# Two DeepNorm layers on one core: where the sums of the feed-forward weights are made

## The chip, the cores and the metric

The kernel runs on one core of one Trainium2 chip. The metric is the device time of one execution in microseconds. Five engines run their own instruction streams in order: PE (TensorE, matmuls), DVE (VectorE), ACT (ScalarE), POOL (GpSimd) and SP (SyncE, which issues most transfers). Sixteen DMA engines, shared by all queues, move data between HBM and on-chip memory. The two queues that matter here are q1 (transfers that SP issues) and q0 (transfers that POOL issues).

## The reference

Two layers over 1024 latent and 256 context tokens, width 1024. Each layer is a modulated input projection, three head groups (latent attention, differential attention, chunk mixing), an output projection with a LayerNorm residual, and a gated feed-forward part with a convolution over three tokens:

```
def conv_ffn(h, p):
    u = dwconv3(h @ p["ffn_wup"], p["ffn_convw"], p["ffn_convb"])
    gate, val = jnp.split(u, 2, axis=-1)
    return (jax.nn.silu(gate) * val) @ p["ffn_wdown"]
...
def layer(x, xc, mod, modc, rows, cols, p, layer_idx, need_ctx):
    ...
    y, yc = mixer(x * (1.0 + sc1) + sh1, xc * (1.0 + csc1) + csh1, rows, cols, p, layer_idx, need_ctx)
    x = layer_norm(DN_ALPHA * x + g1 * y, p["ln1_g"], p["ln1_b"])
    x = layer_norm(DN_ALPHA * x + g2 * conv_ffn(x * (1.0 + sc2) + sh2, p), p["ln2_g"], p["ln2_b"])
```

`ffn_wup` is 1024 x 5632, `ffn_wdown` is 2816 x 1024, all in float32. Layer 1 leaves the context tokens out of its output and feed-forward parts.

## The kernel before

**Numbers.** Each float32 operand is split into a high part (`hi`, type fp32r) and the rest (`lo`), and a product is three matmuls: hi·hi, hi·lo, lo·hi (`mm3`). `split` makes `hi` by a copy on ACT (L460) and `lo` by a subtraction on DVE or POOL (L457).

**The feed-forward part in seven products.** Up and down projections are 2 x 2 block products done with seven block products in place of eight (a Strassen-like scheme), so that sums of weight blocks are needed beside the blocks. For the up projection there are 22 column blocks f (`NF`), and in each the four quarters of the weight, 128 x 512 each, are called 11, 12, 21, 22; S1 = 21 + 22, S2 = S1 + 11, S3 = 21 + 11, S4 = 12 + S2. The products use 11, 12, S1, S2, S3, S4 and 22 (and 21 in layer 0, for the context tokens). For the down projection there are 11 pairs (`NP`) and four sums as well.

**Sums made by transfers.** Before, all of these sums are made in HBM by transfers that POOL issues on q0. `sums` lists them for one layer: a sum of a chunk is a plain copy of one operand (L592) and then a transfer that adds the other operand to what lies there (L593, `accum_op`). Each is 1408 KB, cut in rows of 8 KB for the adding one (176 rows, `SUMROWS`); the sums are called `ws` (up) and `db` (down). `begin_sums` takes the next one of the list and hands it to the planner. This happens in the input projection (`in_chunk`, every fourth tile), among the fillers of the attention (`program`), and in the up phase (`ffn`, L1811). The ws of layer 0 are started in the input projection and the attention of layer 0; the db of layer 0 and half of the ws of layer 1 in the up phase of layer 0; the rest of these in the input projection and the attention of layer 1; the db of layer 1 in the up phase of layer 1.

**The up phase.** For each block f, `up_load` loads the seven or eight weight tiles of 256 KB by SP (L444), four of them from `ws`; `up_operand` splits each on ACT and DVE, `UP_LOOK` = 4 tiles ahead of the product; `up_slot` runs the products on PE and combines them: DVE reads PSUM at L1640 (S2), L1650 (S3) and L1654 (S4), ACT copies the others, and `conv` runs on ACT (L1671) and DVE (L1673). Once in two blocks `store_pair` writes seven combinations of the result to HBM (`da`, `dc`), made by `comb` (L1490) on DVE or POOL. L1650 runs once in each block, so its starts count the blocks.

**What sets the order.** All work goes into `Sched` as tasks with a priority (the order of writing plus `key`), the engines that may take it and a cost; a list scheduler plans it with its own estimates and thereby fixes the order in each engine's stream and the on-chip places ("region" tiles). A POOL transfer counts 1.0 us there and lands 40 us later. On the chip each engine then runs its stream in order and waits by semaphores.

## Time and profile before

| what | value |
| --- | --- |
| median of 3 runs | 3523.48 us (3515.53 to 3527.67) |
| profiled execution | 3522.21 us, its span 3520.4 us |
| granted TensorE clock, mean | 0.957 |
| PE, DVE, ACT, POOL busy | 91%, 73%, 47%, 30% of the span |
| input projection of layer 0, attention | to about 300 us, 300 to 980 us |
| up phase of layer 0, down phase | 985 to 1680 us, 1680 to 2010 us |
| input projection of layer 1, attention | 2010 to 2200 us, 2200 to 2770 us |
| up phase of layer 1, down phase | 2770 to 3257 us, 3257 us to the end |

The span is from the first to the last instruction; the run's time is 1.8 us longer. An instruction's row says which engine ran it, on which line, what it wrote and read, and how long it took; a wait's row says which engine stood still and what ended that. "PE idle" is taken from the rows of PE that carry a wait in brackets. PEclk in a stretch is the TensorE clock that was granted, as a share of full speed; a share of 0.5 is the lower of two levels.

### The profile page before, as it was taken

The numbers are of one execution on the slowest core, as the hardware profiler recorded it, in microseconds if no ns is written. First come the engines' busy times: TensorE is split into PE (matmuls) and PEld (weight loads), VectorE is DVE, ScalarE is ACT, GpSimd is POOL, SyncE is SP. The second block draws the span as 40 slices with busy tenths as digits, with TensorE's granted clock in tenths as the row PEclk, the third lists the DMA queues.
The fourth block names the chain that finished last, engine by engine and source line by source line (L and its number), as shares of the span: only waits on it lengthen the run. The fifth ranks groups of instructions, "written<-read, shape, count | busy, mean of one in ns | idle before, by whom it ended". The sixth has DMA issues, their size and how long they took to land. (4 is left out here: it accounts for less than half of the span.)

```text
span 3520.4 us, 53639 instructions
## 1 busy us (share of the span) xinstructions
PE 3210.6 (91%) x18953; PEld 2801.2 (80%) x18953; DVE 2586.0 (73%) x6262; ACT 1652.2 (47%) x2931; POOL 1045.3 (30%) x678
## 2 busy tenths in 40 slices
PE   7799999998988889989998899999998889999997
PEld 5798888787977777777886799888888867788775
DVE  7456988988777566657569737889898776666687
ACT  5024666565344344434435404566663445454543
POOL 3101555553122111213034301454434232212143
PEclk9899999999999999999999999999998999999998
DMA  8823444443345666664765743132313556653672
GB/s 324 206 65 100 116 120 131 120 106 104 111 145 168 191 176 181 191 173 147 225 217 188 213 130 78 49 77 82 89 53 121 163 157 200 201 163 132 222 263 102
DMA packets 274839, 528.07 MB, mean 150 GB/s; under 512 B 67465, under 2 KB 119177, under 8 KB 264585
## 3 DMA queue, kind: packets, MB, share of 16 engines
q1 hardware_dynamic: 263048, 386.22, 34.1%
q0 software_dynamic: 11520, 138.42, 15.9%
q8 instruction: 149, 2.44, 0.3%
q14 instruction: 122, 0.99, 0.1%
HBM read 444.25 MB, written 218.69 MB: 188 GB/s over the span
## 5 line engine op out<-in xcount | busy, mean ns | idle before, releaser
L447 PE MATMUL t<-region 128*128 128x256 f32 (+4 forms) x15631 | 2876.0, 342 | 233.4 <-DVE region L457 69.7
L447 PEld LDWEIGHTS t<-region 128*128 128x128 f32 x15631 | 2458.0, 194 | 584.9 <-DVE region L457 82.6
L457 DVE TENSOR_TENSOR region<-region 128x512 fp32r<-128x512 f32 (+6 forms) x867 | 765.2, 907 | 267.8 <-ACT region L460 225.0
L460 ACT ACTIVATE region<-t 128x512 fp32r<-128x512 f32 (+4 forms) x935 | 452.6, 511 | 717.1 <-PE t L447 326.0
L460 ACT ACTIVATE region<-region 128x512 fp32r<-128x512 f32 (+4 forms) x944 | 591.2, 662 | 384.8 <-PE t L447 131.9
L457 POOL TENSOR_TENSOR region<-region 128x512 fp32r<-128x512 f32 (+5 forms) x289 | 403.9, 1408 | 1123.2 <-ACT region L460 804.6
L1490 POOL TENSOR_TENSOR region<-region 128x512 f32<-128x512 f32 (+2 forms) x107 | 212.0, 1984 | 911.3 <-ACT region L460 355.2
L1673 DVE SCALAR_TENSOR_TENSOR region<-region,conv 128x1023 f32<-128x1023 f32 x176 | 233.4, 1327 | 165.6 <-ACT region L1671 165.3
L1198 ACT ACTIVATE region<-region,q 128x1280 f32<-128x1280 f32 (+1 forms) x216 | 273.5, 1267 | 165.2 <-DVE q L1197 148.7
L1193 DVE TENSOR_SCALAR_CACHE_REDUCE region<-t 128x512 f32<-128x512 f32 (+1 forms) x600 | 333.6, 586 | 9.4 <-PE t L447 8.0
L457 DVE TENSOR_TENSOR region<-t,region 128x512 fp32r<-128x512 f32 (+1 forms) x529 | 297.8, 598 | 46.4 <-ACT region L460 41.6
L1262 PE MATMUL t<-ident,region 128*128 128x128 f32 x1312 | 186.1, 285 | 19.9 <-DVE region L1193 5.0
L1238 POOL TENSOR_TENSOR region<-region 128x1280 f32<-128x1280 f32 (+1 forms) x69 | 188.4, 2731 | 5.8
L1262 PEld LDWEIGHTS t<-ident,region 128*128 128x128 f32 x1312 | 154.9, 147 | 27.6 <-DVE region L1193 8.2
L1671 ACT ACTIVATE region<-region,conv 128x1024 f32<-128x1024 f32 x88 | 109.2, 1241 | 128.2 <-DVE region L1654 56.7
L1237 POOL TENSOR_SCALAR region<-region,q 128x1280 f32<-128x1280 f32 (+1 forms) x69 | 87.4, 1267 | 205.6 <-DVE q L1232 128.2
L447 PE MATMUL t<-region,s 128*4 128x256 f32 x768 | 118.2, 291 | 17.2 <-ACT region L460 10.8
L1490 DVE TENSOR_TENSOR region<-region 128x512 f32<-128x512 f32 (+2 forms) x150 | 113.3, 760 | 18.4 <-POOL region L1490 15.3
L1018 DVE TENSOR_TENSOR region<-t,region 128x256 f32<-128x256 f32 x32 | 13.6, 424 | 126.5 <-PE t L447 69.6
L447 PEld LDWEIGHTS t<-region,s 128*4 128x4 f32 x768 | 64.8, 87 | 46.4 <-ACT region L460 11.3
L548 POOL TENSOR_TENSOR region<-region 128x1024 f32<-128x1024 f32 x26 | 72.8, 2815 | 93.3 <-DMA region<-n 65.6
L1688 ACT ACTIVATE region<-region 128x1024 f32<-128x1024 f32 x66 | 53.4, 839 | 63.9 <-DVE region L1673 63.9
(137 smaller groups left out, 1849.5 us busy)
## 6 DMA issues: line engine op xcount, KB each, us to landing
ws<-in_wup POOLq DMA_DIRECT2D x48, 1408.0 KB, 9.8
region<-ws SPq DMA_DIRECT2D x176, 256.0 KB, 3.7
region<-in_ada_w SPq DMA_DIRECT2D x160, 256.0 KB, 3.5
region<-in_wup SPq DMA_DIRECT2D x154, 256.0 KB, 3.0
da<-region SPq DMA_DIRECT2D x154, 256.0 KB, 3.7
region<-da SPq DMA_DIRECT2D x154, 256.0 KB, 4.0
db<-in_w_down POOLq DMA_DIRECT2D x24, 1408.0 KB, 8.5
ws<-ws POOLq DMA_DIRECT2D x16, 1408.0 KB, 14.3
```

The lines of the kernel that those rows point to most:

```text
L447: self.nc.tensor.matmul(ps, a, b, start=start, stop=stop, skip_group_check=again)
L457: eng.tensor_tensor(out=out, in0=full, in1=hi.bitcast(F32), op=ALU.subtract)
L460: self.nc.scalar.activation(out, in_, AF.Copy, **kw)
L548: self.task(engs or pool_t(D), lambda e, row=row, op=op: self.vec[e].tensor_tensor(out=x[:, :D], in0=x[:, :D], in1=row.t, op=op), [x, row] ...
L1193: self.task(dve_t(b - a), lambda e: nc.vector.tensor_scalar(p[:, a:b], ps[:, :b - a], -scale, None, op0=ALU.mult, op1=ALU.min, accum_out=n ...
L1198: self.task(act_t(nk, 0.19), lambda e: nc.scalar.activation(p[:, :nk], p[:, :nk], AF.Exp, bias=m.t, scale=-1.0, accum_out=s.t), [p, m], [p ...
L1237: nc.gpsimd.tensor_scalar(p2[:, :nk], p2[:, :nk], cc.t, 0.0, op0=ALU.mult, op1=ALU.add)
L1238: nc.gpsimd.tensor_tensor(out=p1[:, :nk], in0=p1[:, :nk], in1=p2[:, :nk], op=ALU.add)
L1262: nc.tensor.transpose(ps[:, u, j * P:(j + 1) * P], B[key][j][:, (kt + u) * P:(kt + u + 1) * P], self.ident)
L1490: self.task(either(n), lambda e: self.vec[e].tensor_tensor(out=o(), in0=a(), in1=b(), op=op), r, w, **kw)
L1671: self.task(act_t(n, 0.15), lambda e: nc.scalar.activation(t.t, u(0, n), AF.Identity, scale=c[:, 1:2], bias=c[:, 3:4]), r + ["conv"], [t])
L1673: self.task(dve_t(n - 1, extra=0.06), lambda e, d=d: nc.vector.scalar_tensor_tensor(t[:, 1 - d:n - d], u(d, n - 1 + d), c[:, 2 * d:2 * d + ...
```

## The change

The sums of the up projection's weights are no longer made in HBM: `ws` is gone. `up_load` loads the four quarters of each block once (11 and 12 as before; 21 and 22 when S1 is due), and `up_operand` makes S1 to S4 by four additions of 128 x 512 on DVE (`comb`, which is L1480 in the changed file), keeping the quarters and the sums S1 and S2 on chip until their last use. The split of each operand is as before. The down projection's sums are still made by transfers from POOL, now in rows of 2 KB (704 rows in a transfer of the same 1408 KB, for the plain copies too), all 16 of a layer among the fillers of that layer's attention. The room for POOL's descriptors is doubled (`dynamic_dma_scratch_size`).

```diff
-SUMROWS = 176
+SUMROWS = 704
...
     def flat(self, x, c):
-        return x.rearrange("n p c -> (n p c)").rearrange("(r c) -> r c", c=2048)[c * SUMROWS:(c + 1) * SUMROWS]
+        return x.rearrange("n p c -> (n p) c")[c * SUMROWS:(c + 1) * SUMROWS]
...
-            out.append(lambda: self.s.add({"pool": 1.0}, lambda e: self.nc.gpsimd.dma_start(out=put(), in_=self.flat(a(), c)), (), **kw))
-            out.append(lambda: self.s.add({"pool": 1.0}, lambda e: self.nc.gpsimd.dma_start(out=put(), in_=self.flat(b(), c), accum_op=ALU.add, max_dma_last_dim=8192), [*r, key], **kw))
-        for c in range((NF if which == "ws" else NP) * P * 512 // (SUMROWS * 2048)):
-            at = lambda n: (which, l, n, c)
-            if which == "ws":
-                make(0, c, w(1, 0), w(1, 1))
-                make(2, c, w(1, 0), w(0, 0))
-                make(1, c, w(0, 0), lambda: x[0], [at(0)])
-                make(3, c, w(0, 1), lambda: x[1], [at(1)])
-            else:
-                make(0, c, w(0, 0), w(0, 1))
...
+            out.append(lambda: self.s.add({"pool": 1.0}, lambda e: self.nc.gpsimd.dma_start(out=put(), in_=self.flat(a(), c), max_dma_last_dim=2048), (), **kw))
+            out.append(lambda: self.s.add({"pool": 1.0}, lambda e: self.nc.gpsimd.dma_start(out=put(), in_=self.flat(b(), c), accum_op=ALU.add, max_dma_last_dim=2048), [*r, key], **kw))
+        for c in range(NP * P // SUMROWS):
+            at = lambda n: ("db", l, n, c)
+            make(0, c, w(0, 0), w(0, 1))
+            make(1, c, w(0, 1), w(1, 1))
+            make(2, c, w(1, 1), lambda: x[0], [at(0)])
+            make(3, c, w(1, 0), lambda: x[2], [at(2)])
...
-        for n, t in enumerate(tiles):
-            if name != "z" and n % 4 == 1:
-                self.begin_sums(1)
+        for t in tiles:
...
     def up_load(self, l, m):
-        while len(self.up_raw) <= min(m, len(self.up_ops) - 1):
-            f, n = self.up_ops[len(self.up_raw)]
-            raw = self.S(F32, (P, HALF))
-            if n[0] == "S":
-                j = int(n[1]) - 1
-                src, r = self.ws[l][j, f], self.sum_chunks("ws", l, j, f)
-            else:
-                src, r = self.i["wup"][l, int(n[0]) - 1, int(n[1]) - 1, f], []
-            self.dma(lambda raw=raw: raw.t, lambda src=src: src, 4 * P * HALF, r, [raw])
-            self.up_raw.append(raw)
+        while self.up_loaded <= min(m, len(self.up_ops) - 1):
+            f, n = self.up_ops[self.up_loaded]
+            self.up_loaded += 1
+            for g, h in {"11": [(0, 0)], "12": [(0, 1)], "S1": [(1, 0), (1, 1)]}.get(n, ()):
+                raw = self.S(F32, (P, HALF))
+                self.dma(lambda raw=raw: raw.t, lambda f=f, g=g, h=h: self.i["wup"][l, g, h, f], 4 * P * HALF, (), [raw])
+                self.up_raw[f, g, h] = raw
...
-        raw, self.up_raw[m] = self.up_raw[m], None
-        self.blocks[f][n] = self.parts(HALF, lambda: raw.t, [raw], engs=dve_t(HALF))
+        b = self.blocks[f]
+        raw = lambda g, h: self.up_raw[f, g, h]
+        if n[0] == "S":
+            x, y = {"S1": lambda: (raw(1, 0), raw(1, 1)), "S2": lambda: (b["s1"], raw(0, 0)), "S3": lambda: (raw(1, 0), raw(0, 0)), "S4": lambda: (raw(0, 1), b["s2"])}[n]()
+            t = b[n.lower()] = self.S(F32, (P, HALF))
+            self.comb(HALF, lambda: t.t, lambda: x.t, lambda: y.t, ALU.add, [x, y], [t], engs=dve_t(HALF))
+        else:
+            t = raw(int(n[0]) - 1, int(n[1]) - 1)
+        b[n] = self.parts(HALF, lambda: t.t, [t], engs=dve_t(HALF))
...
-        assert not self.due
-        self.due = self.sums(l, "db") + (self.sums(1, "ws") if l == 0 else [])
...
-            if f >= 2 and (x[1] == "22" or l == 0 and f % 2 and x[1] == "S2"):
-                self.begin_sums(1)
...
-        self.due = self.sums(0, "ws")
         for l in range(DEPTH):
...
+            self.due = self.sums(l)
...
-    nc = _bacc.Bacc("TRN2", target_bir_lowering=False, num_devices=1, dynamic_dma_scratch_size=1024)
+    nc = _bacc.Bacc("TRN2", target_bir_lowering=False, num_devices=1, dynamic_dma_scratch_size=2048)
```

The next three places show what the planner made of it. The first is POOL's stream in the middle of the up phase of layer 0. L1490 (L1480 in the changed file) is an addition or subtraction of `comb`, L592 the plain copy of a sum and L593 the adding transfer. Before:

```order
L1490 TENSOR_TENSOR region<-region 128x1024
L1490 TENSOR_TENSOR region<-region 128x512
L593 DMA db<-db 176x2048
L1490 TENSOR_TENSOR region<-region 128x1024
L592 DMA ws<-in_wup 32x11264
L593 DMA db<-db 176x2048
L1490 TENSOR_TENSOR region<-region 128x1024
L1490 TENSOR_TENSOR region<-region 128x512 x2
L592 DMA ws<-in_wup 32x11264
L593 DMA ws<-in_wup 176x2048
```

The same place now:

```order
L1480 TENSOR_TENSOR region<-region 128x128
L1480 TENSOR_TENSOR region<-region 128x512 x2
L1480 TENSOR_TENSOR region<-region 128x1024 x2
L1480 TENSOR_TENSOR region<-region 128x128
L1480 TENSOR_TENSOR region<-region 128x512 x2
```

No transfer is left in POOL's stream between the start of the up phase and the next attention, and of the combinations of `store_pair` POOL takes one of 128 columns more in a pair of blocks and fewer of 512.

The second place is DVE's stream in the same phase, from the combination S4 of one block (L1654, now L1648) to the splits for the next. L1673 (now L1667) is the convolution and L457 the `lo` part of an operand. Before:

```order
L1654 TENSOR_TENSOR region<-region,t 128x512
L1673 SCALAR_TENSOR_TENSOR region<-region,conv 128x1023
L1673 SCALAR_TENSOR_TENSOR region<-t,conv,region 128x255
L1673 SCALAR_TENSOR_TENSOR region<-region,conv 128x1023
L1673 SCALAR_TENSOR_TENSOR region<-t,conv,region 128x255
L457 TENSOR_TENSOR region<-region 128x512 x2
L1673 SCALAR_TENSOR_TENSOR region<-region,conv 128x1023
```

Now:

```order
L1648 TENSOR_TENSOR region<-region,t 128x512
L1480 TENSOR_TENSOR region<-region 128x512
L1667 SCALAR_TENSOR_TENSOR region<-region,conv 128x1023
L1667 SCALAR_TENSOR_TENSOR region<-t,conv,region 128x255
L1667 SCALAR_TENSOR_TENSOR region<-region,conv 128x1023
L1667 SCALAR_TENSOR_TENSOR region<-t,conv,region 128x255
L457 TENSOR_TENSOR region<-region 128x512
L1480 TENSOR_TENSOR region<-region 128x512
L457 TENSOR_TENSOR region<-region 128x512
L1480 TENSOR_TENSOR region<-region 128x512
```

The additions stand in the gaps between convolution and splits, two to four places ahead of the split that reads them; in each block DVE has 8 splits as before and 4 more instructions of this kind.

The third place is POOL's stream in the attention of layer 1. L1237 and L1238 (now L1227 and L1228) join the two maps of the differential attention. Before:

```order
L1237 TENSOR_SCALAR region<-region,q 128x1280
L1238 TENSOR_TENSOR region<-region 128x1280
L593 DMA ws<-ws 176x2048
L457 TENSOR_TENSOR region<-region 128x512 x3
L457 TENSOR_TENSOR region<-region 128x2x2x32 x2
```

Now:

```order
L1227 TENSOR_SCALAR region<-region,q 128x1280
L1228 TENSOR_TENSOR region<-region 128x1280
L592 DMA db<-in_w_down 704x512
L591 DMA db<-in_w_down 704x512
L457 TENSOR_TENSOR region<-region 128x768
L457 TENSOR_TENSOR region<-region 128x512 x2
```

From the first filler to the last, this attention has 16 transfers in POOL's stream where it had 4, and in a few places, as here, two stand one behind the other.

## Rows read from the trace of the kernel before

**Rows 1.** The page: the queue of POOL's transfers (packets, MB, share of 16 engines' span), and the issues of POOL and of the up phase's loads (how many, size of each, median time from issue to landing).

```profile
q0 software_dynamic: 11520, 138.42, 15.9%
...
ws<-in_wup POOLq DMA_DIRECT2D x48, 1408.0 KB, 9.8
region<-ws SPq DMA_DIRECT2D x176, 256.0 KB, 3.7
region<-in_wup SPq DMA_DIRECT2D x154, 256.0 KB, 3.0
db<-in_w_down POOLq DMA_DIRECT2D x24, 1408.0 KB, 8.5
ws<-ws POOLq DMA_DIRECT2D x16, 1408.0 KB, 14.3
db<-db POOLq DMA_DIRECT2D x8, 1408.0 KB, 13.0
```

**Rows 2.** Windows, one row a stretch: its length, busy time of PE, its weight loads, DVE, ACT and POOL with the number of instructions, then the granted clock, the DMA engines' busy share and GB/s. They are: the stall in the input projection of layer 0, the attention of layer 0, the up phase of layer 0 (the part with sums under way, then the part after the last of them), the up phase of layer 1 (its opening, then the rest).

```profile
150.00:170.00 20.00, 3.07 (x27) 2.87 (x25) 0.00 (x0) 0.00 (x0) 2.09 (x3) 0.64 1.04 258
300.00:980.00 680.00, 628.13 (x4524) 570.06 (x4523) 578.88 (x1813) 391.50 (x762) 281.83 (x198) 0.96 0.41 116
1094.00:1580.00 486.00, 432.53 (x2168) 363.68 (x2167) 290.38 (x367) 189.02 (x305) 86.11 (x60) 0.95 0.65 185
1580.00:1651.00 71.00, 66.50 (x343) 55.79 (x342) 50.72 (x61) 32.98 (x55) 14.96 (x8) 1.00 0.40 124
2797.00:2900.00 103.00, 84.38 (x385) 70.31 (x385) 73.24 (x80) 49.38 (x82) 32.79 (x20) 0.88 0.61 176
2900.00:3257.00 357.00, 350.01 (x1505) 281.73 (x1504) 237.83 (x275) 177.84 (x266) 73.83 (x36) 1.00 0.57 174
```

**Rows 3.** The instructions of L1650, one in each block of the up phase, in four stretches: count, shortest, median and longest duration in ns, start of the first and of the last. The stretches are 1094 to 1580 and 1600 to 1655 (layer 0), 2890 to 3260 and 3085 to 3240 (layer 1).

```profile
L1650 DVE SCALAR_TENSOR_TENSOR region<-t,region x17: 682/686/692, 1094.3 to 1570.5; 128x512 f32<-128x512 f32 x17
...
L1650 DVE SCALAR_TENSOR_TENSOR region<-t,region x3: 691/692/692, 1600.8 to 1651.0; 128x512 f32<-128x512 f32 x3
...
L1650 DVE SCALAR_TENSOR_TENSOR region<-t,region x19: 682/684/692, 2897.2 to 3256.8; 128x512 f32<-128x512 f32 x19
...
L1650 DVE SCALAR_TENSOR_TENSOR region<-t,region x8: 682/684/685, 3102.2 to 3238.9; 128x512 f32<-128x512 f32 x8
```

**Rows 4.** The timeline of one block of the up phase of layer 0, POOL, ACT, DVE and PE in turn: start, busy time, instruction, and in brackets the engine's idle time before it and what ended that.

```profile
1290.28 2.40 POOL L1490 TENSOR_TENSOR region<-region 128x1024 f32<-128x1024 f32 x1 [23.27 <-ACT region L460]
1292.63 0.55 POOL L592 DMA_DIRECT2D ws<-in_wup  x1
1293.17 0.93 POOL L593 DMA_DIRECT2D db<-db  x1
...
1307.63 0.63 ACT L460 ACTIVATE region<-region 128x512 fp32r<-128x512 f32 x1 [9.56 <-DMA region<-in_wup]
...
1290.44 2.78 DVE L457 TENSOR_TENSOR region<-region 128x512 fp32r<-128x512 f32 x1
...
1308.29 0.69 DVE L457 TENSOR_TENSOR region<-region 128x512 fp32r<-128x512 f32 x1 [10.91 <-ACT region L460]
...
1309.64 10.55 PE L447 MATMUL t<-region 128*128 128x512 f32 x52 [7.09 <-DVE region L1650]
```

**Rows 5.** Waits in the input projection of layer 0, 110 to 175 us: who waited for whom, us in total, how often, the longest.

```profile
DVE region L1018 <- DMA zd<-region: 39.8, 1, 39.8
POOL ws L593 <- issue: 24.8, 4, 7.8
...
PE t L447 <- DVE region L1024: 19.4, 1, 19.4
```

**Rows 6.** The timeline where the input projection of layer 1 begins, POOL, ACT and PE in turn, columns as in rows 4.

```profile
1992.47 0.96 POOL L593 DMA_DIRECT2D ws<-in_wup  x1
...
2006.87 0.84 ACT L460 ACTIVATE region<-region 128x768 fp32r<-128x768 f32 x1 [16.83 <-DMA region<-in_w_in_dv]
...
2011.92 10.25 PE L447 MATMUL t<-region 128*128 128x64 f32 x47 [10.66 <-DVE q L499]
```

**Rows 7.** The timeline of the beginning, ACT and PE, columns as in rows 4.

```profile
74.54 1.27 ACT L460 ACTIVATE region<-region 128x1280 fp32r<-128x1280 f32 x1 [6.11 <-DMA region<-in_w_in_dk]
...
83.99 1.94 PE L447 MATMUL t<-region 128*128 128x64 f32 x8 [6.72 <-issue]
90.34 19.84 PE L447 MATMUL t<-region 128*128 128x64 f32 x94 [4.41 <-issue]
```

**Rows 8.** Groups of DVE's instructions in the up phase of layer 0 (980 to 1680 us) and, last, of layer 1 (2770 to 3240 us): count, busy us and mean ns of one, idle time before them.

```profile
L457 DVE TENSOR_TENSOR region<-region 128x512 fp32r<-128x512 f32 x195 | 193.3, 1006 | 112.5 <-ACT region L460 99.9 <-issue 6.6 <-DMA region<-ws 3.4
...
L1654 DVE TENSOR_TENSOR region<-region,t 128x512 f32<-128x512 f32 x22 | 14.9, 682 | 1.7 <-PE t L447 1.7
...
L457 DVE TENSOR_TENSOR region<-region 128x512 fp32r<-128x512 f32 x164 | 139.1, 868 | 29.4 <-ACT region L460 28.8 <-PE t L447 0.4
```

**Rows 9.** POOL's transfers in the attention of layer 0 (300 to 980 us): duration on POOL in ns, shortest, median and longest, and their time from issue to landing; then the wait of PE for POOL's joins there.

```profile
L592 POOL DMA_DIRECT2D ws<-in_wup x7: 553/581/587, 352.2 to 689.7; - x7
L593 POOL DMA_DIRECT2D ws<-in_wup x4: 867/902/907, 304.5 to 624.3; - x4
...
DMA to landing us min/median/max: 6.0/9.9/10.9
...
PE t L1262 <- POOL region L1238: 0.8, 1, 0.8
```

More of the change, by code (lines that the diff above doesn't have):

```diff
@@ L577, in flat, with sums @@
     def flat(self, x, c):
-        return x.rearrange("n p c -> (n p c)").rearrange("(r c) -> r c", c=2048)[c * SUMROWS:(c + 1) * SUMROWS]
-    def sums(self, l, which):
-        src = self.i["wup" if which == "ws" else "w_down"]
-        x = (self.ws if which == "ws" else self.db)[l]
-        w = lambda a, b: (lambda: src[l, a, b])
+        return x.rearrange("n p c -> (n p) c")[c * SUMROWS:(c + 1) * SUMROWS]
+    def sums(self, l):
+        x = self.db[l]
+        w = lambda a, b: (lambda: self.i["w_down"][l, a, b])
         out = []
         def make(n, c, a, b, r=()):
-            key = (which, l, n, c)
+            key = ("db", l, n, c)
             put = lambda: self.flat(x[n], c)
             kw = dict(w=[key], key=MODKEY, late=40.0)
-            out.append(lambda: self.s.add({"pool": 1.0}, lambda e: self.nc.gpsimd.dma_start(out=put(), in_=self.flat(a(), c)), (), **kw))
-            out.append(lambda: self.s.add({"pool": 1.0}, lambda e: self.nc.gpsimd.dma_start(out=put(), in_=self.flat(b(), c), accum_op=ALU.add, max_dma_last_dim=8192), [*r, key], **kw))
-        for c in range((NF if which == "ws" else NP) * P * 512 // (SUMROWS * 2048)):
-            at = lambda n: (which, l, n, c)
-            if which == "ws":
-                make(0, c, w(1, 0), w(1, 1))
-                make(2, c, w(1, 0), w(0, 0))
-                make(1, c, w(0, 0), lambda: x[0], [at(0)])
-                make(3, c, w(0, 1), lambda: x[1], [at(1)])
-            else:
-                make(0, c, w(0, 0), w(0, 1))
-                make(1, c, w(0, 1), w(1, 1))
-                make(2, c, w(1, 1), lambda: x[0], [at(0)])
-                make(3, c, w(1, 0), lambda: x[2], [at(2)])
+            out.append(lambda: self.s.add({"pool": 1.0}, lambda e: self.nc.gpsimd.dma_start(out=put(), in_=self.flat(a(), c), max_dma_last_dim=2048), (), **kw))
[6 more added lines that the diff above has]
+            make(3, c, w(1, 0), lambda: x[2], [at(2)])
         return out
@@ L616, in sum_chunks @@
         a, b = f * P * 512, (f + 1) * P * 512 - 1
-        m = SUMROWS * 2048
+        m = SUMROWS * 512
         return [(name, l, n, c) for c in range(a // m, b // m + 1)]
@@ L683, in setup @@
         self.dc = d.tile([7, P, NP, P], F32, tag="dc", name="dc")
-        self.ws = [d.tile([4, NF, P, HALF], F32, tag=f"ws{l}", name="ws") for l in range(DEPTH)]
         self.db = [d.tile([4, NP, P, HALF], F32, tag=f"db{l}", name="db") for l in range(DEPTH)]
@@ L1367, in out_begin @@
         self.s.what = f"wo{l}"
-        self.up_raw, self.up_ops = [], [x[:2] for x in self.up_order(l) if len(x) == 3 and x[2] != 1]
+        self.up_raw, self.up_loaded, self.up_ops = {}, 0, [x[:2] for x in self.up_order(l) if len(x) == 3 and x[2] != 1]
         self.blocks, self.up_made = [{} for _ in range(NF)], 0
@@ L1476, in out_half, with comb @@
         return sm
-    def comb(self, n, o, a, b, op, r, w, **kw):
-        self.task(either(n), lambda e: self.vec[e].tensor_tensor(out=o(), in0=a(), in1=b(), op=op), r, w, **kw)
+    def comb(self, n, o, a, b, op, r, w, engs=None, **kw):
+        self.task(engs or either(n), lambda e: self.vec[e].tensor_tensor(out=o(), in0=a(), in1=b(), op=op), r, w, **kw)
     def parts(self, n, full, r, w=None, engs=None):
```

## The prediction

> **What bounds the kernel now.** I read the windows by stage first, to see who is busy where; then the waits of PE in the stages where it is not; then the timeline of one such wait. PE is busy for 628 of 680 us of the attention and 350 of 357 us late in layer 1's up phase [rows 2], so it sets the end, and what a change is worth is the time in which PE stands or runs slowly. The up phase of layer 0 is the place to look. While transfers from POOL are under way there, PE is busy 433 of 486 us at a granted clock of 0.95; after the last of them it is busy 66.5 of 71 us at 1.00 [rows 2]. The same shows in the pace of the blocks: 17 starts of L1650 lie 476.2 us apart, 29.8 us a block, against 25.1 us for the last ones, and 20.0 us in layer 1 against 19.5 us late in it [rows 3].
>
> The timeline shows how the time is lost. POOL issues a plain copy and an adding transfer at 1292.6 and 1293.2; 1.4 MB each then occupies the DMA engines. ACT waits 9.6 us for a weight tile that SP had asked for just then, DVE stands 10.9 us behind ACT's split, and L1650 is queued on DVE behind that `lo` part although its own operands are there. PE waits 7.1 us for L1650 [rows 4]. A weight tile lands in 3.0 us in the median, the sums take 8.5 to 14.3 us [rows 1]. The same thing happens where the input projection of layer 0 begins: DVE waits 39.8 us for a store to leave its buffer, and PE stands 19.4 us [rows 5] with the DMA engines fully busy and every other engine empty [rows 2]. And where that of layer 1 begins: ACT waits 16.8 us for a weight, PE 10.7 us [rows 6].
>
> **The change part by part.** The sum is made against the profiled execution, 3522.2 us, which is 1.3 us under the median.
>
> *Up phase, layer 0: sums go, loads shrink.* All 30 transfers of POOL leave this stage, and SP's loads go from 176 + 154 = 330 [rows 1] to 176 (4 a block, 22 blocks, 2 layers), 40 MB less. If every block then runs like the last ones, 16 blocks gain 29.8 - 25.1 = 4.7 us each, 75 us, and the block from 1570.5 to 1600.8 (30.3 us) gains 5: 80 us [rows 3].
>
> *Up phase, layer 0: four additions a block on DVE.* The nearest rows are `lo` parts of the same size with both inputs on chip: 1.006 us in the mean [rows 8]; the combination with one input in PSUM takes 0.682 us, which I take for the bare length. So 2.7 to 4.0 us a block. DVE is busy 290 of 486 us, 17.8 us a block; with the additions 20.5 to 21.8 of 25.1 us, still not full. But it works in order, and the products wait for splits that now stand behind an addition. That costs between nothing and 4.0 us a block (all of it on the path); I take 0.5 us, near the low end, since the idle time of a block (7 us) is about twice the additions: 20 blocks, 10 us. Sum for this stage -70 us, bounds -80 and 0. In the opening, with two blocks side by side and DVE dense, I add 3 us (0 to 8, eight additions of 1.0 us).
>
> *Input projection of layer 0.* With no sum left before the attention the store leaves as other stores do and the 19.4 us of PE go [rows 5]; the clock, which was at 0.64 in that stretch because PE had stood [rows 2], gives about 2 us more: -21 us (-19 to -22). At the very beginning five copies compete with the weights of the next projection: ACT waits 6.1 us for one, and PE has two gaps of 6.7 and 4.4 us soon after [rows 7]. PE's work there hangs on DVE as well, so I take 5 of these 11 us (0 to 11).
>
> *Input projection of layer 1.* The 16.8 us for the weight shrink to a usual landing, and 10.7 us of PE go [rows 6]: -11 us (0, if the statistics on DVE end late anyway, to -14 with the clock).
>
> *Up phase, layer 1.* From 2897.2 to 3102.2 the ten blocks take 20.5 us each, and with no sums left 19.5 us [rows 3]: -10 us. In the opening PE is busy 84 of 103 us at 0.88 with DVE at 71% [rows 2]; shorter loads help there and twelve additions of 0.87 us [rows 8] hurt; I set it at -3. The additions afterwards: DVE goes from 238/357 x 20.0 = 13.3 to 16.0 to 16.8 us of 19.5; at 0.3 us a block +5 us. Together -8 us (-20 to +10).
>
> *Attention: the transfers of 2 KB rows.* Layer 0 has 16 for some 15, layer 1 16 where there were 4; none of rows of 2 KB is in the trace. On POOL a plain copy takes 0.55 to 0.58 us and an adding one 0.90 us [rows 9]. The page has 11520 packets for 96 issues [rows 1], 120 in the mean, and the adding ones have 176 rows each, so the copies have 64. If the difference of 0.33 us is that of 112 pieces, it is 3 ns a piece, and 704 pieces take 2.5 us. Bounds: 0.9 us (nothing for pieces) and 3.6 us (four times as much). Taken 2.5, that is 16 x 1.8 = 28 us more on POOL in a stage where it is busy 282 of 680 us and PE waits for its joins 0.8 us [rows 2, 9]. Behind each issue stand `lo` parts and joins, which PE needs a few us later. I count +3 us in layer 0. In layer 1 twelve more transfers land in 10 us each beside loads that PE needs; at half a microsecond each +6 us. Bounds -5 and +40.
>
> The Trainium skill ("DMA: Bandwidth & Descriptors", Anatomy of one DMA — SWDGE (gpsimd) path) puts descriptor generation down as small and says that many can be emitted before it shows. By that the issue would stay near 0.9 us, and the sum 3 us lower. Rows 9 speak for a small slope; neither row reaches 704.
>
> Sum: -70 + 3 - 21 - 5 - 11 - 8 + 3 + 6 = -103, so 3522.2 - 103 = **3419 us**.
>
> **The rivals.** *A, the additions meet POOL.* Beside a POOL operation of 2.40 us, a `lo` part on DVE took 2.78 us in place of 0.68 [rows 4], and the mean of 1.006 us [rows 8] says that this is common. If the additions cost 1.5 us in the mean, DVE needs 23.8 of 25.1 us in layer 0 and 19.3 of 19.5 in layer 1, and I give up 1 us a block more in 20 blocks of layer 0 and 0.7 us in 18 of layer 1: 3419 + 20 + 13 = 3452 us. The Trainium skill ("SBUF — State Buffer", Who interferes with whom) has this as a rule: a DVE instruction with two inputs in SBUF and a POOL instruction that reads SBUF exclude each other for the length of one. The rows agree (2.78 beside 2.40 us).
>
> *B, the same, with DVE as the new bound: slower than before.* If each addition waits out a POOL operation, 2.78 us, DVE needs 17.8 + 11.1 = 28.9 us a block in layer 0 and 13.3 + 11.1 = 24.4 us in layer 1. Then layer 0 gains 0.9 x 20 = 18 in place of 70, and layer 1 loses 4.4 x 18 = 79: 3419 + 52 + 87 = 3558 us. It decides from about (19.5 - 13.3)/4 = 1.55 us for an addition, where layer 1 turns. Against it: POOL is busy only 74 of 357 us there, 4.1 us a block [rows 2], and cannot block more than that.
>
> *C, POOL stands at its issues.* In the input projection of layer 0 POOL waits four times, 6.2 us each, before an adding transfer with nothing that the profile names [rows 5]. If room for pieces is what is missing, rows of 2 KB bring it back: 32 issues x 6.2 = 198 us on POOL, and if a third reaches PE through late joins, 3419 + 66 = 3485 us. Against it: in the attention before, no such wait is seen beside the transfers [rows 9], and the room is doubled; for it, pieces are four times as many and some issues stand one behind the other.
>
> *D, the sums were not the cause.* The stores of `da` and the loads are in these blocks as well; if those make the wait, nothing goes: 3522 us. Against it: the last blocks have the same stores and loads and run at 25.1 us [rows 3].
>
> **How the numbers follow.** The forecast (3385 to 3450) has 0.62, A 0.15, C 0.09, B 0.07, D 0.05, and 0.02 is left for better than 3385. The range 3385 to 3485 holds the forecast, A and C, 0.86 in all; the bounds of the up phase and of the attention do not fall together. Faster by over 0.3% (about 10 us, what a measurement of this kernel can tell): 0.62 + 0.15 + 0.09 + 0.02 = 0.88. Within 0.3%: D, 0.05. Slower: B, 0.07.
>
> **What would show it.** In the changed kernel the combination S3 of DVE should start every 25 to 26 us through all of layer 0's up phase and every 19.5 to 20 us in layer 1's, with ACT waiting for weight tiles next to nothing. The gaps of 19.4 and 10.7 us should be gone. The additions should take 0.7 to 1.0 us; 1.5 us or more speaks for A or B. POOL's issues should take 2 to 3 us; idle time of 5 us or more before them speaks for C. Wrong would be the whole if the pace of layer 0's blocks stayed at 29 us, or if the attention of layer 1 grew by more than 30 us.

## The result and the profile after

The changed kernel takes 3410.43 us (median of 4 runs, 3408.78 to 3411.25), the one before 3524.36 us (median of 4): a ratio of 0.968, 95% interval 0.9662 to 0.9698. The profiled execution has a span of 3409.5 us against 3520.4, so the traces differ by 110.9 us. The forecast was 3419 us, -103.

Where the time went is read from instructions that stand in both programs: the start of one before minus its start after is the lead that the changed kernel has there, and the growth of the lead over a stage is what the stage gave. The last instances of the combination S3, for example, start at 1651.0 [rows 3] and 1561.4 us, a lead of 89.6 us.

| stage, by the clock of before | forecast | measured | lead at its end |
| --- | --- | --- | --- |
| beginning, to 127 us | -5 | -2.9 | 2.9 |
| input projection of layer 0, to 236 us | -21 | -21.4 | 24.3 |
| attention of layer 0, to 972 us | +3 | +8.4 | 15.9 |
| up phase of layer 0, opening, to 1094 us | +3 | +6.3 | 9.6 |
| the rest of it, to 1651 us | -70 | -80.0 | 89.6 |
| down phase of layer 0, to 1970 us | none | -3.5 | 93.1 |
| input projection of layer 1, to 2145 us | -11 | -6.1 | 99.2 |
| attention of layer 1, to 2751 us | +6 | -7.0 | 106.2 |
| up phase of layer 1, to 3257 us | -8 | -5.3 | 111.5 |
| the end | none | +0.6 | 110.9 |

Windows of the changed kernel, columns as in [rows 2]: the place of the former stall, the attention of layer 0, the up phase of layer 0 after its opening, then the up phase of layer 1, opening and rest.

```profile
150.00:170.00 20.00, 20.00 (x173) 20.00 (x173) 0.00 (x0) 2.81 (x8) 0.00 (x0) 1.00 0.14 47
300.00:965.00 665.00, 606.62 (x4382) 552.70 (x4381) 557.16 (x1754) 385.14 (x744) 274.02 (x185) 0.95 0.38 108
1084.00:1561.00 477.00, 477.00 (x2510) 407.80 (x2509) 380.40 (x502) 230.11 (x360) 83.14 (x46) 1.00 0.29 89
2690.00:2790.00 100.00, 83.30 (x374) 66.72 (x375) 82.27 (x96) 49.42 (x81) 31.12 (x17) 0.90 0.15 48
2790.00:3145.00 355.00, 348.33 (x1510) 282.17 (x1509) 301.49 (x330) 184.07 (x268) 96.53 (x45) 1.00 0.30 99
```

PE is busy in all of the 477 us of layer 0's loop at full clock, where it was 433 of 486 us at 0.95 [rows 2]; the stall of 19.4 us is gone. DVE has more to do in both up phases: 380 us of 477, and 301 of 355 in layer 1.

The starts of S3 (L1644, once L1650), columns as in [rows 3]; layer 0 after the opening, layer 1 after the opening, and the last eight blocks of layer 1.

```profile
L1644 DVE SCALAR_TENSOR_TENSOR region<-t,region x20: 690/692/692, 1084.7 to 1561.4; 128x512 f32<-128x512 f32 x20
...
L1644 DVE SCALAR_TENSOR_TENSOR region<-t,region x19: 676/691/693, 2789.4 to 3145.3; 128x512 f32<-128x512 f32 x19
...
L1644 DVE SCALAR_TENSOR_TENSOR region<-t,region x8: 676/684/693, 3005.3 to 3145.3; 128x512 f32<-128x512 f32 x8
```

Layer 0's blocks take (1561.4 - 1084.7)/19 = 25.1 us each, the pace that the last ones had before; layer 1's take 19.8 us, and the last eight 20.0, where the last ones before took 19.5.

The additions in the up phase of layer 0 (L1480 on DVE, with some of `store_pair`): shortest, median and longest duration in ns.

```profile
L1480 DVE TENSOR_TENSOR region<-region x142: 275/679/694, 1088.3 to 1554.7; 128x512 f32<-128x512 f32 x95, 128x128 f32<-128x128 f32 x28, 128x256 f32<-128x256 f32 x19
```

An addition takes 0.68 us, its bare length. In layer 1 the same group has a longer mean (2790 to 3145 us; count, busy us, mean ns):

```profile
L1480 DVE TENSOR_TENSOR region<-region 128x512 f32<-128x512 f32 x80 | 78.9, 986 | 0.3
```

In the trace 18 of these 80 run beside a POOL operation and take 2.03 us in the mean; the other 62 take 0.68.

The transfers on POOL, all 32, columns as in [rows 9]; in the changed file L591 is the plain copy and L592 the adding transfer:

```profile
L591 POOL DMA_DIRECT2D db<-in_w_down x16: 692/725/872, 222.1 to 2416.3; - x16
L592 POOL DMA_DIRECT2D db<-in_w_down x8: 1100/1148/1176, 263.3 to 2323.7; - x8
L592 POOL DMA_DIRECT2D db<-db x8: 1117/1126/1165, 409.8 to 2463.9; - x8
```

And POOL's waits ahead of them, from 250 to 2500 us (what ended the wait by the profile, us in total, how often, the longest):

```profile
POOL db L591 <- issue: 23.4, 2, 13.2
POOL db L591 <- DMA oT<-region: 12.9, 1, 12.9
POOL db L591 <- DVE q L1187: 8.5, 1, 8.5
```

The issues are cheap (0.73 and some 1.13 us), but four copies are preceded by waits of 8.5 to 13.2 us. In each case an adding transfer stands just ahead in POOL's stream, and the copy goes 0.3 us after that one has landed; when the other twelve copies are issued, the transfer before them has landed, and they don't wait. For example, the adding transfer of 552.57 lands 14.0 us later, at 566.6, and the copy goes at 566.89. Two of the waits bear other names; those engines had no part in it, as the experiments show. The timeline of POOL there, and PE's row (columns as in [rows 4]):

```profile
552.57 1.13 POOL L592 DMA_DIRECT2D db<-in_w_down  x1
566.89 0.71 POOL L591 DMA_DIRECT2D db<-in_w_down  x1 [13.20 <-issue]
567.61 5.21 POOL L457 TENSOR_TENSOR region<-region 128x512 fp32r<-128x512 f32 x4
...
570.41 1.51 PE L1117 MATMUL t<-identr,region 128*128 128x128 f32 x10 [7.46 <-POOL region L457]
```

PE waits 7.46 us for a `lo` part queued on POOL behind the copy; the same happens at 423.4 (6.55 us), and in layer 1 at 2291.6 (5.0 us). This is rival C, in 4 of 32 issues.

### The profile page after: what moved, and what is told of

Read it like the earlier page. It is cut to its first block, busy times and chain, and to the rows that moved or that the text cites. A ratio compares the mean times of both kernels' runs of the same rounds, so it can differ in the third digit from the quotient of the medians.

```text
span 3409.5 us, 53373 instructions
## 1 busy us (share of the span) xinstructions
PE 3186.5 (93%) x18953; PEld 2785.7 (82%) x18953; DVE 2700.5 (79%) x6407; ACT 1677.3 (49%) x2944; POOL 1028.0 (30%) x631
## 5 line engine op out<-in xcount | busy, mean ns | idle before, releaser
L447 PE MATMUL t<-region 128*128 128x512 f32 (+4 forms) x15631 | 2853.0, 341 | 137.8 <-DVE region L457 55.0
L457 DVE TENSOR_TENSOR region<-region 128x512 fp32r<-128x512 f32 (+6 forms) x873 | 760.0, 893 | 176.2 <-ACT region L460 122.7
L460 ACT ACTIVATE region<-t 128x512 fp32r<-128x512 f32 (+4 forms) x948 | 462.1, 514 | 600.0 <-PE t L447 386.3
L457 POOL TENSOR_TENSOR region<-region 128x512 fp32r<-128x512 f32 (+7 forms) x283 | 392.3, 1398 | 1109.3 <-ACT region L460 714.8
L1480 POOL TENSOR_TENSOR region<-region 128x512 f32<-128x512 f32 (+3 forms) x132 | 248.6, 1889 | 823.6 <-DVE region L1667 518.5
L457 DVE TENSOR_TENSOR region<-t,region 128x512 fp32r<-128x512 f32 (+1 forms) x529 | 296.9, 595 | 52.8 <-ACT region L460 50.9
L1667 DVE SCALAR_TENSOR_TENSOR region<-region,conv 128x1023 f32<-128x1023 f32 x176 | 231.6, 1325 | 36.7 <-ACT region L1665 36.5
L1480 DVE TENSOR_TENSOR region<-region 128x512 f32<-128x512 f32 (+3 forms) x301 | 226.3, 770 | 2.5 <-DMA da<-region 1.4
L1228 POOL TENSOR_TENSOR region<-region 128x1280 f32<-128x1280 f32 (+1 forms) x68 | 186.8, 2746 | 5.7
L1227 POOL TENSOR_SCALAR region<-region,q 128x1280 f32<-128x1280 f32 (+1 forms) x68 | 84.5, 1242 | 210.6 <-DVE q L1222 137.7
L548 DVE TENSOR_TENSOR region<-region 128x1024 f32<-128x1024 f32 x34 | 62.3, 1841 | 18.2 <-DMA region<-n 17.7
```

The source lines that it names most:

```text
L447: self.nc.tensor.matmul(ps, a, b, start=start, stop=stop, skip_group_check=again)
L457: eng.tensor_tensor(out=out, in0=full, in1=hi.bitcast(F32), op=ALU.subtract)
L460: self.nc.scalar.activation(out, in_, AF.Copy, **kw)
L548: self.task(engs or pool_t(D), lambda e, row=row, op=op: self.vec[e].tensor_tensor(out=x[:, :D], in0=x[:, :D], in1=row.t, op=op), [x, row] ...
L1227: nc.gpsimd.tensor_scalar(p2[:, :nk], p2[:, :nk], cc.t, 0.0, op0=ALU.mult, op1=ALU.add)
L1228: nc.gpsimd.tensor_tensor(out=p1[:, :nk], in0=p1[:, :nk], in1=p2[:, :nk], op=ALU.add)
```

## The experiments

The theory: the transfers of the sums delayed the loads and stores of the up phase (and of both input projections), and moving them away gave the time; what the change took back is the waits of POOL for room. The rivals: the number of loads, the size of the transfers' pieces, and the price of the additions. Times are medians of 4 runs; the ratio is to the kernel before, on the same chip.

**Room for two transfers** (e2, and less room, e3).

```diff
-dynamic_dma_scratch_size=2048
+dynamic_dma_scratch_size=4096
```

> The changed kernel with dynamic_dma_scratch_size 4096 in place of 2048 and nothing else. Theory R: the four waits of POOL at its issues (8.5 to 13.2 us) go, PE's 19 us behind them go, the issues still take 0.7 and 1.1 us: 3392 to 3400 us. Rival Q (the copy waits for the adding transfer ahead of it in any case): no change, 3410 us, the waits as they were.

Measured: 3386.21 us (3384.48 to 3392.41), ratio 0.9619 (0.96 to 0.9637). No transfer of POOL has a wait ahead of it any more, the issues take 0.73 and 1.12 us as before, and the lead over the changed kernel grows by 20 us in layer 0's attention and 8 in layer 1's, of which 3 are lost again in the up phase behind it. Q falls: more room alone removes the waits. It gives 24 us, somewhat more than PE's 19 us of named waits.

```diff
-dynamic_dma_scratch_size=2048
+dynamic_dma_scratch_size=1536
```

> The changed kernel with dynamic_dma_scratch_size 1536 in place of 2048 and nothing else. Theory R: less room, so an adding transfer waits behind a copy still under way as well, and the waits of POOL at its issues get more or longer than the four of the changed kernel (44.8 us in all); the time rises by 0 to 15 us, 3410 to 3425. Rival Q: the same four waits, 3410 us.

Measured: 3412.58 us (3405.84 to 3415.78), ratio 0.9684 (0.9662 to 0.9706), with the same four waits, 45.6 us in all against 44.8. No adding transfer waits behind a copy, so the further waits that R allowed for did not come; by itself this run does not tell R from Q.

**Rows of 8 KB in the attention** (e1).

```diff
-SUMROWS = 704
+SUMROWS = 176
...
-in_=self.flat(a(), c), max_dma_last_dim=2048
+in_=self.flat(a(), c)
...
-accum_op=ALU.add, max_dma_last_dim=2048
+accum_op=ALU.add, max_dma_last_dim=8192
```

> The changed kernel with the pieces of the down sums as before (rows of 8 KB for the adding transfers, 64 pieces for the copies); every stream has the same order. In the changed kernel POOL stands four times (10.2, 13.2, 12.9, 8.5 us) before a plain copy that follows an adding transfer, each time until that transfer has landed, and PE waits 14.0 us in layer 0 and 5.0 us in layer 1 for `lo` parts queued behind. Theory R (the pieces of two transfers do not fit into POOL's room): with 176 pieces the four waits go, the issues take 0.55 and 0.90 us again, PE's 19 us go: 3392 to 3400 us. Rival Q (a copy behind an adding transfer waits whatever its pieces): the waits stay and so does the time, 3410 us. Rival P (the rows of 2 KB are what makes the transfers harmless for loads and stores): the waits go but PE gets new gaps behind loads; 3410 or more.

Measured: 3404.2 us (3396.63 to 3410.46), ratio 0.9666 (0.9644 to 0.9687). The waits are gone here too, so R holds; but 18 us are missing against the kernel with room for 2 KB rows, which has no such waits either: 12 us in the attention of layer 0 and 5 in that of layer 1, by the leads. The two differ in the pieces, and in room that neither waits for, so P has these. Beside larger pieces the loads that the attention needs come later: the loads of `in_ada_w` in the attention of layer 0, who waited for them, and their time to landing, first with rows of 8 KB:

```profile
  ACT region L460: 10.9, 4
...
DMA to landing us min/median/max: 2.4/3.1/16.0
```

and with rows of 2 KB and room 4096:

```profile
  ACT region L460: 1.0, 1
...
DMA to landing us min/median/max: 2.5/3.2/8.5
```

**The first part of the change alone** (e6). The down sums go back into the up phase, pieces as before the change:

```diff
+            if f >= 2 and x[1] == "22":
+                self.begin_sums(1)
...
-            fill += [lambda: self.begin_sums(1)] * (...)
-SUMROWS = 704
+SUMROWS = 176
```

> The changed kernel with the down sums put back into the up phase (one in each block from the third on, pieces as before the change), so only the up sums' part of the change is done: the loads are 4 a block and the additions are on DVE, but 16 transfers run in each up phase. Theory T (1.4 MB transfers delay the loads and stores of the up phase): the pace of layer 0's blocks goes from 25.1 to 27 or 28 us while they run, some 16 blocks, so 30 to 45 us; layer 1's goes from 19.8 to 20.5, 10 us; the attentions give back up to 19 us of POOL's waits: 3425 to 3450 us. Rival L (the number of loads was the cause, not the transfers): the pace stays at 25.1 us, and the time is 3392 to 3405.

Measured: 3473.72 us (3463.02 to 3479.14), ratio 0.986 (0.9836 to 0.9884). So the up sums' part alone is worth 47 us, and what was done with the down sums 63. L falls. T's mechanism holds, but the loss is 24 us over its range: 45 us are lost in layer 0's up phase, the upper end, 26 in layer 1's where 10 were expected, and 12 about the beginning of layer 1's attention. Blocks with an adding transfer and a copy take 31 us, those without 24.9. The timeline of one (POOL, SP's queue, ACT, DVE, PE in turn; columns as in [rows 4]):

```profile
1227.50 0.92 POOL L592 DMA_DIRECT2D db<-in_w_down  x1
...
1232.68 0.57 POOL L591 DMA_DIRECT2D db<-in_w_down  x1
...
1238.10 0.33 SPq L444 DMA_DIRECT2D region<-in_wup  x1
...
1244.92 0.63 ACT L460 ACTIVATE region<-region 128x512 fp32r<-128x512 f32 x1 [11.03 <-DMA region<-in_wup]
1245.59 0.69 DVE L457 TENSOR_TENSOR region<-region 128x512 fp32r<-128x512 f32 x1 [8.36 <-ACT region L460]
...
1252.23 8.04 PE L447 MATMUL t<-region 128*128 128x512 f32 x34 [1.71 <-DVE region L457]
```

It is the chain of [rows 4] again, load to ACT to DVE, now with 4 loads a block; PE's waits from 1060 to 1560 us come to 30 of the 45 us, and the granted clock there is 0.97 to 0.98 in place of 1.00. SP's loads stand in one stream with the stores of `da` and `dc`; a store of `da` lands in 12.6 us in the median beside a transfer, in 3.1 us otherwise (20 and 50 of them in this phase).

**The pieces of 2 KB alone** (e8), in the kernel before, all 96 transfers in place, with room 4096:

```diff
-SUMROWS = 176
+SUMROWS = 704
...
-dynamic_dma_scratch_size=1024
+dynamic_dma_scratch_size=4096
```

> The kernel before with rows of 2 KB for all its 96 transfers of sums, copies too, in the same places of the same streams, and dynamic_dma_scratch_size 4096: the second part of the change alone, without its move. A load's packets share the DMA engines with packets of 8 and 44 KB before, of 2 and 4 KB now. Theory S (it is the size of the pieces ahead of a load's or store's packets that delays it): layer 0's pace comes down from 29.8 to 26 or 27 us, the 19.4 us gap of the input projection mostly goes; 3440 to 3465 us. Rival V (it is the bytes: the transfers keep the DMA engines full however they are cut): the pace stays at 28.5 us or more; 3495 to 3530.

Measured: 3447.19 us (3441.3 to 3452.51), ratio 0.978 (0.9748 to 0.9813): two thirds of the change's gain without moving any transfer to another place. Layer 0's blocks take (1597.0 - 1071.8)/19 = 27.6 us, in place of 29.3 over the same 20 blocks [rows 3]; the input projection's gap of 19.4 us is gone. The time is in S's range, the pace falls less than S said. Which of the two, pieces or room, does it was not separated here: POOL waited at its issues before as well [rows 5]. How long the store behind that gap takes to land can be read. All transfers of `zd` from 50 to 300 us in the kernel before:

```profile
DMA to landing us min/median/max: 1.7/1.8/47.3
```

and in e8:

```profile
DMA to landing us min/median/max: 1.7/6.1/14.8
```

The longest is a store both times, and in e8 the median is worse. In the changed kernel the last of these stores is issued at 202.4 us and the first sum at 222.1; its longest store takes 3.7 us.

**Rows of 2 KB in the up phase of the changed kernel** (e9): the kernel of e6 with SUMROWS 704 and room 4096.

> The kernel of e6 (down sums in the up phase, additions on DVE) with rows of 2 KB and dynamic_dma_scratch_size 4096; the order of all streams is that of e6. e6 lost some 45 us in layer 0's up phase and 26 in layer 1's against the changed kernel, 31 us for a block with a copy and an adding transfer against 24.9 without. Theory S (the size of the pieces ahead of a load's packets): blocks with transfers come down to 26 to 28 us, 3415 to 3440. Rival V (the bytes): 30 us or more, 3460 to 3475.

Measured: 3465.0 us (3462.86 to 3468.21), ratio 0.9833 (0.9814 to 0.9852). V holds in layer 0: blocks with transfers take 30 to 35 us, the loop (1594.1 - 1068.1)/19 = 27.7 us a block against 27.5 in e6. There a store of `da` beside a transfer still takes 10.2 us to land in the median, against 12.7 (1060 to 1600 us). In layer 1 the traces say otherwise: 18 blocks take 20.1 us each, against 20.9 in e6 and 19.8 in the changed kernel, so the finer cut or the room gives back 15 of the 20 us lost there. The medians of the whole, 3465.0 and 3473.7 us, are too close to settle more. Why the finer cut helped in e8 and in layer 1, and not in layer 0 here, stays open.

**No transfers at all** (e5) in the kernel before; its loads stay seven or eight a block, and those of the down sums' tiles are replaced in the same way:

```diff
-        for f in self.due[:n]:
-            f()
...
-                src, r = self.ws[l][j, f], self.sum_chunks("ws", l, j, f)
+                src, r = self.i["wup"][l, j // 2, j % 2, f], []
```

> The kernel before with all 96 transfers of the sums left out; the tiles that came from the sums are loaded from a quarter of the weight in place (so the sums are left out of the computation, up and down), and no addition is made on DVE. It has 330 loads in the up phases as before. Theory T (the transfers themselves are what delays loads and stores): layer 0's blocks start every 25 us, the gaps of 19.4 and 10.7 us are gone, and with neither additions nor POOL's waits the time is 3375 to 3395 us. Rival L (the seven or eight loads a block are a good part of it): the pace stays at 26 us or more and the time is over 3405.

Measured: 3386.37 us (3382.18 to 3387.99), ratio 0.9606 (0.9578 to 0.9635). All 96 transfers cost 136 us. Layer 0's blocks take (1548.3 - 1067.9)/19 = 25.3 us with 330 loads in the up phases. The changed kernel, with 176, takes 25.1, and without its additions (e4, below) 25.4: the loads saved are worth nothing that can be told from the planner's choice of order.

**No additions** (e4) in the changed kernel:

```diff
-            x, y = {"S1": lambda: (raw(1, 0), raw(1, 1)), ...}[n]()
-            t = b[n.lower()] = self.S(F32, (P, HALF))
-            self.comb(...)
+            t = {"S1": raw(1, 1), "S2": raw(0, 0), "S3": raw(1, 0), "S4": raw(0, 1)}[n]
```

> The changed kernel without its additions: S1 to S4 are not made, and their splits read a quarter of the weight as it was loaded (so the four sums are left out of the computation); loads, splits and products are as many as before. Theory N (the additions lie beside PE's work in layer 0, where the blocks already start every 25.1 us, and cost some 0.5 us a block late in layer 1 and a few us in the openings): 3395 to 3406 us, layer 1's late pace back at 19.5 us, layer 0's still 25.1. Rival F (the terms as forecast, 10 + 3 us in layer 0 and some 10 in layer 1, are all on the path): 3385 to 3390. Rival Z (nothing): 3410.

Measured: 3395.72 us (3392.23 to 3397.26), ratio 0.9633 (0.9605 to 0.9662), 15 us under the changed kernel: N. Layer 0's loop gains nothing: with the order planned anew a block takes (1559.9 - 1077.2)/19 = 25.4 us, and the 6 us lost there eat most of the 7.5 us gained up to the end of layer 0's opening. Layer 1's goes from 19.8 to (3129.5 - 2779.5)/18 = 19.4 us, some 6 us, and its opening gives some 8.

**The additions elsewhere** (e7, e10, e11, e12). All of them on POOL:

```diff
-ALU.add, [x, y], [t], engs=dve_t(HALF))
+ALU.add, [x, y], [t], engs=pool_t(HALF))
```

> The changed kernel with its four additions a block on POOL in place of DVE (the planner orders the rest anew). POOL's combinations of 128 x 512 take 1.3 to 1.9 us, so 5 to 8 us a block, and POOL is busy some 5 us a block now. Theory N (DVE has room in layer 0 and little in layer 1, 83% busy late there): layer 0's pace stays 25.1 us, layer 1's late pace comes back to 19.5 us, 3400 to 3412 us. Rival X (POOL's operations lengthen DVE's splits, whose mean is 1.0 us now against 0.68 alone, by more than the additions cost DVE): the splits' mean rises to 1.3 us or more and the time to 3415 to 3450.

Measured: 3438.48 us (3437.06 to 3441.14), ratio 0.9756 (0.9722 to 0.9791). The time is in X's range, but the splits' mean stays under X's 1.3 us: in layer 1's loop they go from 0.912 to 0.994 us, and the convolution on DVE from 1.279 to 1.509 us. DVE's row of it and POOL's additions (mean ns):

```profile
L1667 DVE SCALAR_TENSOR_TENSOR region<-region,conv 128x1023 f32<-128x1023 f32 x72 | 107.4, 1509 | 25.1 <-ACT region L1665 24.8
...
L1480 POOL TENSOR_TENSOR region<-region 128x512 f32<-128x512 f32 x92 | 150.9, 1650 | 215.5 <-DMA region<-in_wup 52.4 <-DVE region L1480 41.8 <-DVE region L1667 35.3
```

How much of the 28 us comes from the longer operations on DVE, and how much from the additions' own 1.65 us, for which the splits wait, was not separated.

Three more were made on top of room 4096:

```diff
+engs=either(HALF))
```

> The changed kernel with dynamic_dma_scratch_size 4096 (3386 us by itself) and the additions open to DVE or POOL, as the planner finds room. Leaving the additions out gave 15 us: about 3 in layer 0's opening, 8 in layer 1's, 6 late in layer 1. Theory N (DVE's room there is what they cost): part of it comes back, 3374 to 3384 us. Rival X (a POOL operation lengthens DVE's splits by as much): 3386 to 3410.

```diff
+engs=pool_t(HALF) if f < UP_FIRST[l] else dve_t(HALF))
```

> The changed kernel with dynamic_dma_scratch_size 4096 and the additions of the openings alone (two blocks of layer 0, three of layer 1, 20 additions) on POOL. Theory N: DVE is the crowded engine in the openings (97 of 122 us in layer 1's), so the lead that e4 had there, 3 and 8 us, comes back in part: 3376 to 3384 us. Rival X: POOL takes over twice as long for one and is crowded there too (37 of 122 us, with its splits queued behind): 3386 to 3400.

```diff
+engs=pool_t(HALF) if l and n == "S4" else dve_t(HALF))
```

> The changed kernel with dynamic_dma_scratch_size 4096 and one addition of four (S4) on POOL in layer 1. DVE is busy 133.6 of 160 us late in layer 1's up phase, where a block takes 20.0 us against 19.5 before. Theory N (DVE's load sets that): the late pace falls to 19.6 to 19.8 us and the time by 4 to 8 us, 3378 to 3382. Rival X (the additions on POOL hold DVE up, as where all were on POOL, when blocks alternated between 17.8 and 22.2 us): the pace stays at 20 us or more, 3386 to 3400.

Measured: 3395.82 us (3392.99 to 3397.94), ratio 0.9638 (0.9616 to 0.9659) for `either`, 10 us behind its base of 3386.21, in X's range; 3390.42 us (3385.92 to 3397.21), ratio 0.9622 (0.9599 to 0.9644) for the openings, not to be told from the base, so N falls there; and 3378.43 us (3371.38 to 3384.67), ratio 0.9586 (0.9562 to 0.9609) for S4. In the S4 run PE is busy in all of layer 1's loop (the window, columns as in [rows 2]), and 18 starts of S3 (under it) lie 326.4/17 = 19.2 us apart, better than N expected:

```profile
2770.00:3120.00 350.00, 349.88 (x1526) 286.57 (x1525) 297.83 (x341) 184.21 (x268) 85.39 (x36) 1.00 0.32 102
...
L1644 DVE SCALAR_TENSOR_TENSOR region<-t,region x18: 691/692/693, 2791.6 to 3118.0; 128x512 f32<-128x512 f32 x18
```

The pace in the trace is clear; that the whole is better than room 4096 alone is likely and not settled, since the two intervals touch. It is the best version seen: 32 us under the changed kernel, of which room gives 24.

But N's reason, DVE's load, is not what fell: from 2763 to 3118 us DVE is busy 303 of 355 us, as much as in the changed kernel, since the planner put wider combinations of `store_pair` on it. The run with the openings on POOL says it more plainly. Its loops have all four additions on DVE, and in layer 1 the blocks start every (3128.8 - 2781.7)/18 = 19.3 us, with DVE busy 301 of 355 us (2773 to 3128). The starts, and the additions with their mean, 0.71 us in place of 0.99:

```profile
L1644 DVE SCALAR_TENSOR_TENSOR region<-t,region x19: 676/691/692, 2781.7 to 3128.8; 128x512 f32<-128x512 f32 x19
...
L1480 DVE TENSOR_TENSOR region<-region 128x512 f32<-128x512 f32 x82 | 58.3, 711 | 0.9 <-DMA region<-in_wup 0.5
```

In return its splits there take 1.03 us in place of 0.91. So the pace in layer 1 hangs on the order that the planner finds, not on DVE's share alone. What this run wins in its loops it loses elsewhere, some of it in layer 1's opening.

## Why the prediction was right, point by point

**The cause** was the one forecast: with the transfers gone layer 0's blocks run at 25.1 us (e5: 25.3 without any transfer, seven or eight loads; e6: 27.5 with 16 transfers, four loads). "Loads shrink" added nothing that the runs can tell.

**The up phase of layer 0** was worth 80 us, the full term before additions were charged. The charge of 10 us for them was the step mis-sized: they cost nothing in the loop (e4), since each took 0.68 us in time that DVE had left. The opening cost 6 us, forecast 3; e4, in an order of its own, puts the additions' share at some 7, inside the 0 to 8 allowed. Rivals A and B fell here: no addition in layer 0's loop took longer than 0.69 us. In layer 1 they took 0.986 us in the mean, between the bare length and A's 1.5: A's mechanism is there, in 18 of 80 additions. The loop gave 111.5 - 107.8 = 3.7 us in place of 5 there (the lead at 2897 was 107.8).

**The input projections:** -21.4 for -21; in layer 1 -6.1 for -11, inside the bounds. PE's wait there was shortened only, to 4.7 us for a statistic on DVE, the lower end that the prediction named.

**The attentions** are the term that was wrong in its reason, and that they came out near their forecast, +1.4 us together for +9, was luck. The price of pieces was not the mechanism. A copy is issued in 0.73 us, an adding one in 1.13 us, not 2.5: 528 rows more cost an adding transfer 1.13 - 0.90 = 0.23 us, 0.4 ns each where 3 ns were forecast. That had been drawn from a count of 64 pieces in a copy; the packets of the trace show 32 of 44 KB, the rest being the small ones that every issue brings. The rule of the Trainium skill ("DMA: Bandwidth & Descriptors", Anatomy of one DMA — SWDGE (gpsimd) path), that generation is small, fits the trace here. What did cost was rival C, held unlikely because the room was doubled: 24 us by e2, against 66 in its price. It was met in four places of 32 because there alone a copy stands close behind an adding transfer.

Two gains that the prediction did not have hid it. In layer 0 the +8.4 us are 20 us of C and a gain of 12: with room (e2) this attention is 12 us shorter than before the change, with no transfers in it (e6) 12 us as well, and with as many transfers in rows of 8 KB and no waits (e1) as long as before. So with these streams transfers in pieces of 8 and 44 KB cost 12 us there and those of 2 and 4 KB nothing; with the streams of the kernel before, e8's finer pieces gain nothing in this stage. In layer 1 the forecast was +6 and -7 was measured. The kernel before has PE waiting 2.8 and 1.8 us at 2185 and 2204 us; in the changed kernel these two waits are gone. Windows of the same place before, now, and in e6, whose attention of layer 1 holds no transfers and which has the two waits again (columns as in [rows 2]):

```profile
2150.00:2200.00 50.00, 45.82 (x279) 42.10 (x278) 31.52 (x123) 22.57 (x57) 5.17 (x5) 0.90 0.49 122
...
2051.00:2101.00 50.00, 48.62 (x338) 46.50 (x337) 34.91 (x133) 24.50 (x63) 6.39 (x7) 1.00 0.67 158
...
2070.00:2120.00 50.00, 45.77 (x265) 41.93 (x264) 30.42 (x129) 20.98 (x55) 4.39 (x4) 0.90 0.29 86
```

e6 loses 12 us there against the changed kernel. That speaks for the order that the planner found with the fillers; which step of it fills the gap was not tried.

**Up phase of layer 1:** -5.3 for -8. The late blocks take 0.5 us longer than before, where 0.3 was forecast for the additions, and without them (e4) they take 19.5 us again. The reason given, that DVE has too little room, is not borne out: the run with the openings on POOL has the same additions on DVE, as busy as here (301 of 355 us), and 19.3 us a block.

**The pieces.** The prediction took rows of 2 KB for a cost alone. They are a gain in the attentions (e1 against e2, 18 us); in e8 they gave 75 us together with more room, none of it in layer 0's attention. The Trainium skill ("DMA: Bandwidth & Descriptors", Queues, rings and completion order) says that a DMA engine takes turns between queues packet by packet; the longest store of `zd`, 47.3 us beside packets of 8 and 44 KB and 14.8 us beside 2 and 4 KB, agrees with that, and layer 0 of e9 shows that this is not all.

## What to carry to other kernels

Bulk transfers that no one waits for are paid by those loads and stores that someone does wait for: price them by the pace of the stage with and without them, not by the engine that issues them. Where they must run, try them in another stage and cut finer, and give the issuing engine room for all pieces under way, since what stands behind a waiting issue may be what PE needs. A share of busy time does not say what work handed to an engine costs: with DVE 85% busy, the same four additions a block went with 19.8 us a block in one order and 19.3 us in another. And where a stage comes out near its forecast, look whether two errors cancel: 20 us of waits and a gain of 12 stood behind +8.4.

## What was not expected of the hardware

POOL stands at an issue until an earlier transfer has landed when its room is short: with 704 rows in the adding transfer and 352 packets in the copy, it does so at a `dynamic_dma_scratch_size` of 2048 and of 1536, but not at 4096, and with 176 and 32 not at 2048. The profile gives such a wait no cause ("issue"), or a chance one (`oT`, `q`). And a finer cut costs the issue next to nothing: four times the rows, 0.23 us more.
